# Down projection of a decoder step: twenty of its 43 row blocks by seven products, conv inputs loaded earlier

## The chip, the cores and the metric

The kernel runs on one core of one Trainium2 chip. The metric is the device time of one execution in microseconds (us), lower is better. TensorE (PE in the rows) does the matmuls, VectorE (DVE) and ScalarE (ACT) the elementwise work, GpSimd (POOL) some elementwise work and the DMAs that its software issues, and SyncE (SP) issues most of the other DMAs.

## The reference

One layer of a hybrid decoder for 544 tokens (512 of a prompt, 8 times 4 samples), width 2048, all in float32. A mixer (gated linear attention in 10 heads, dilated attention in 12) ends in an output projection and a residual `h`. Then comes the feed-forward part that the change is about, and a last RMSNorm:

```
up   = rmsnorm(h) @ w_up                    # 2048 -> 2 x 5504
conv = conv_b + sum(conv_w[j] * full[:, j:j+t] for j in 0..2)   # causal, width 3, history from state_ffn_conv
u, g = conv[..., :5504], conv[..., 5504:]
h    = h + (silu(g) * u) @ w_down           # 5504 -> 2048
y    = rmsnorm(h) * norm_final
```

The product with `w_down` has 43 blocks of 128 rows to sum over (k), 16 output tiles of 128 features (ot), and 544 tokens in two halves of 272.

## The kernel before

Every float32 operand is cut into a rounded high part (`hi`, by ACT) and a remainder (`lo`, by DVE: source minus `hi`); `split` does it (L190, L191). One product of a 128x128 weight block with 272 tokens is then three matmuls: hi*hi, hi*lo, lo*hi. Weights come as `raw` tiles of up to eight k blocks by DMA on SP and are split into `whi` and `wlo`, of which there are three buffers each; of `raw` there are three too.

The order of the stages is: input projection with the attention (to about 840 us of the span), output projection (`w_out`, to about 1061), up projection with conv and SiLU (to about 1985), down projection (the rest). A scheduler orders each engine's instructions by itself: blocks under `high_priority` (`ahead`, `evac`) are put forward by so many instructions, and a pool gives a buffer away only when its last reader is done. Each engine, and SP's and POOL's issuing of DMAs, runs its list strictly in order.

**Output projection.** The 16 normed head outputs `o[k]` are split into `ah`/`al` pairs (`act_pair`, one fixed buffer pair for each number); the pairs are those that held the input of the layer, which the last input tile still reads, k = 0 first. `order` sums o[10] to o[15] first. The residual rows `h` are loaded by POOL (L935) and added to the PSUM tile `g`, of which there are two.

**Up projection.** It already uses seven products instead of eight (Strassen's scheme in Winograd's form) for each pair of output tiles, pair of k blocks and the two token halves: `factors` makes seven right factors of the activations (B11, B21, B22, T1 to T4), `Pair` loads and adds the weight blocks. Sums of two weight blocks are made by a second DMA from POOL that adds into the tile (`accum_op`), others by DVE (L1013, L1034). `ra` and `rs` are the tiles of the first block and of the sum, with buffers of their own; the other three loads of a pair use `raw`. Before the first pair's conv, POOL loads `vcv` (conv weights, L1086) and `ci` (conv history, L1101) into the pool `FP`.

**Down projection.** The activations of each k block went to DRAM (`adr`), but for the three blocks of KEPT. The three KEPT blocks are multiplied first for all 16 tiles (L225, evacuated by ACT at L1156). The other 40 follow in groups of 16, 16 and 8: `fetch` loads a block into `ar` (L1141) and splits it into `dh`/`dl`, `gemm` (L225) runs over the group for each of the 16 tiles, DVE adds the PSUM tile to `h[ot]` (L1199) and, in the first group, the residual `hr` (L1203). Of the last group, the second eight tiles are done half by half so that the final norm of the first half runs beside the second.

Of the kernel before, what the change touches and what calls it, by code (L numbers as in the profile page):

```python
# [17 lines left out]
P = 128  # L18
# [27 lines left out]
NSLOT = 11  # L46
# [77 lines left out]
def _build(tc, nc, es, xT, st_gla, ck, cv, conv_in, vecs, w_in, w_gu, w_out, w_up, w_dn,  # L124
# [744 lines left out]
    for k in order:  # L869
        og[k] = act_pair(k)  # L870
        split(og[k][0], og[k][1], o[k])
# [23 lines left out]
    def factors(some, X, pool):  # L895
# [24 lines left out]
        for i in some:  # L920
            nc.vector.scalar_tensor_tensor(b[i][:, 2], b[i][:, 0], -1.0, b[i][:, 2], op0=OP.mult, op1=OP.subtract)
            if late:
                parts(i, T4, 1, b[i][:, 2:3])
            else:
                parts(i, T3, 2, b[i][:, 1:3])

# [158 lines left out]
    vcv = FP.tile([P, NVEC - V_CW], F32, name="vcv")  # L1085
    nc.gpsimd.dma_start(vcv, vecs[:, V_CW:])  # L1086

    ci_v = conv_in.rearrange("p (s f) r -> p s f r", s=2)
    co_v = conv_out.rearrange("p (s f) r -> p s f r", s=2)
# [5 lines left out]
    ci = co = None  # L1095
    for f, pr in enumerate(pairs):
        if f % 4 == 0:
            n = min(4, KF - f)
            ci = FP.tile([P, 2, 4, 2 * NB], F32, tag="ci", name="ci", bufs=2)
            co = FP.tile([P, 2, 4, 2 + 2 * NB], F32, tag="co", name="co", bufs=2)  # L1100
            nc.gpsimd.dma_start(ci[:, :, :n, :], ci_v[:, :, f:f + n, :])  # L1101
# [27 lines left out]
    ds_p, DS = opened(name="ds", bufs=NSLOT)  # L1129

    taken = [0]

    def slot(n=0):

        pool = DS2 if n else DS
        return pool.tile([P, NT], F32R, tag="dh", name="dh"), pool.tile([P, NT], F32R, tag="dl", name="dl")

    def fetch(k, n):
        hi, lo = slot(n)
        x = DS.tile([P, NT], F32, tag="ar", name="ar", bufs=2)  # L1140
        nc.sync.dma_start(x, adr[k])  # L1141
        split(hi, lo, x)
        return hi, lo

    h = [None] * KD
    A1 = {}
    rest = [k for k in range(KF) if k not in KEPT]
    groups = [rest[:16], rest[16:32], rest[32:]]
    with tc.high_priority(offset=min(1500, tc.cur_priority - P0)):
        for k in groups[0][:NSLOT]:  # L1150
            A1[k] = fetch(k, 0)
# [6 lines left out]
    ds2_p, DS2 = opened(name="ds2", bufs=24 - NSLOT, side="right")  # L1158
    w3_p, W3 = opened(name="w3", bufs=1, side="right")
    even = [0]  # L1160

    def wraw():
        even[0] ^= 1
        if even[0]:
            return wts.tile([P, 8, P], F32, tag="raw", name="raw", bufs=3)
        return W3.tile([P, 8, P], F32, tag="raw3", name="raw3", bufs=2)
# [4 lines left out]
    def wheld(w, ks, c0, n):  # L1171

        raw = wraw()
        wload(raw, w, ks, c0)
        out = []
# [146 lines left out]
```

## Time and profile before

| | |
|---|---|
| median of 3 runs | 2524.89 us (2522.66 to 2529.08) |
| the profiled execution, its own time | 2525.1 us |
| its span, first to last instruction | 2523.3 us |
| PE busy | 2462.7 us, 19479 matmuls |
| DVE, ACT, POOL busy | 1619.3, 1078.8, 435.3 us |
| mean granted TensorE clock | 0.991 of full |

The profiled execution lasted 1.8 us longer than its span and lies 0.2 us above the median. Busy time of PE is an upper bound of its useful time, since matmuls overlap in it; so the argument goes by how many matmuls pass in a stretch, and by the times at which PE waits.

### The profile page before, as it was taken

Reading aid. Unit: us, or ns where it says so; the run is one execution under the profiler, and the core shown is the slowest. Engines: PE = TensorE matmul, PEld = TensorE weight load, DVE = VectorE, ACT = ScalarE, POOL = GpSimd, SP = SyncE. Lnnn points to the kernel's source line nnn. Section 1 sums busy time; section 2 is a strip of 40 time slices with the busy share of each in tenths; the row PEclk is TensorE's granted clock in tenths of the full one; section 3 lists DMA queues with packets and bytes.
Section 4 is the critical chain, followed back from the end, with each engine's and each line's share of the span. In section 5 each row is a group of like instructions: output and inputs, shape, how many; then the busy total and the mean of one; then the engine's idle time right before and its main releaser. Section 6 shows DMA issues by size and latency. Waiting matters only on the chain.

```text
span 2523.3 us, 47163 instructions
## 1 busy us (share of the span) xinstructions
PE 2462.7 (98%) x19479; PEld 2385.2 (95%) x19479; DVE 1619.3 (64%) x2460; ACT 1078.8 (43%) x1870; POOL 435.3 (17%) x581
## 2 busy tenths in 40 slices
PE   8999999999999899989999999999999999999997
PEld 8988887899999899989999999999999999999997
DVE  7777764267777843478878888888888643342243
ACT  6344464133334433355555555555555531131142
POOL 1333434210002320112212221222121000000001
PEclk9999999999999999999999999999999999999999
DMA  7777744544555498668888888889888473443232
GB/s 220 197 202 197 193 114 138 161 131 141 166 177 177 159 305 256 169 146 192 192 188 192 191 191 189 191 191 192 189 191 178 124 219 107 115 151 92 85 100 72
DMA packets 581593, 427.73 MB, mean 170 GB/s; under 512 B 18976, under 2 KB 553728, under 8 KB 580608
## 3 DMA queue, kind: packets, MB, share of 16 engines
q1 hardware_dynamic: 462144, 248.31, 34.9%
q0 software_dynamic: 115200, 171.02, 30.1%
q10 hardware_dynamic: 4032, 5.38, 0.6%
q8 instruction: 153, 2.51, 0.4%
q14 instruction: 64, 0.52, 0.1%
HBM read 397.40 MB, written 77.37 MB: 188 GB/s over the span
## 4 chain that ended last, share of the span: by engine, by line
PE 82%; DMA 8%; DVE 6%; issue 2%; POOL 1%; ACT 1%; SPq 0%; DVEq 0%; POOLq 0%; ACTq 0%
PE g L225 40%; PE b L965 20%; PE g L965 15%; DMA q<-qscr 6%; DVE pr L411 1%; PE v L507 1%; PE s L673 1%; DMA ar<-adr 1%; DVE wlo L191 1%; DVE kv L412 1%; PE s L561 1%; DMA xr<-in_xT_dram 0%; PE s L548 0%; PE s L795 0%; POOL q L408 0%
## 5 line engine op out<-in xcount | busy, mean ns | idle before, releaser
L191 DVE TENSOR_TENSOR wlo<-raw,whi 128x1024 fp32r<-128x1024 f32 (+1 forms) x341 | 408.3, 1198 | 295.6 <-ACT whi L190 288.7
L190 ACT ACTIVATE whi<-raw 128x1024 fp32r<-128x1024 f32 (+1 forms) x345 | 355.0, 1030 | 555.1 <-PE g L225 454.0
L225 PE MATMUL g<-ah,whi 128*128 128x272 f32 x2048 | 442.9, 296 | 9.8 <-ACT ah L190 4.6
L225 PE MATMUL g<-al,whi 128*128 128x272 f32 x2048 | 447.2, 297 | 0.5 <-DVE al L191 0.5
L225 PE MATMUL g<-ah,wlo 128*128 128x272 f32 x2048 | 442.4, 295 | 0.3 <-DVE wlo L191 0.3
L965 PE MATMUL b<-vh,whi 128*128 128x272 f32 x1376 | 395.1, 288 | 6.2 <-ACT V L1038 4.8
L965 PE MATMUL b<-vl,whi 128*128 128x272 f32 x1376 | 395.9, 289 | 0.8 <-DVE vl L893 0.6
L965 PE MATMUL b<-vh,wlo 128*128 128x272 f32 x1376 | 389.9, 288 | 1.3 <-DVE wlo L191 1.3
L225 PEld LDWEIGHTS g<-ah,whi 128*128 128x128 f32 x2048 | 327.9, 191 | 19.7 <-issue 10.3
L225 PEld LDWEIGHTS g<-al,whi 128*128 128x128 f32 x2048 | 329.2, 191 | 11.6 <-issue 9.3
L225 PEld LDWEIGHTS g<-ah,wlo 128*128 128x128 f32 x2048 | 328.3, 190 | 10.2 <-issue 8.5
L965 PE MATMUL g<-vl,whi 128*128 128x272 f32 x1032 | 298.8, 290 | 2.0 <-DVE vl L893 1.9
L965 PE MATMUL g<-vh,whi 128*128 128x272 f32 x1032 | 297.8, 289 | 0.4 <-ACT vh L892 0.3
L965 PE MATMUL g<-vh,wlo 128*128 128x272 f32 x1032 | 296.8, 288 | 0.0
L965 PEld LDWEIGHTS b<-vh,whi 128*128 128x128 f32 x1376 | 260.0, 189 | 6.7 <-ACT V L1038 5.1
L225 PE MATMUL g<-dh,whi 128*128 128x272 f32 x1248 | 258.0, 288 | 4.1 <-ACT whi L190 2.7
L965 PEld LDWEIGHTS b<-vl,whi 128*128 128x128 f32 x1376 | 259.5, 189 | 1.5 <-DVE vl L893 1.5
L965 PEld LDWEIGHTS b<-vh,wlo 128*128 128x128 f32 x1376 | 257.4, 189 | 1.5 <-DVE wlo L191 1.5
L225 PE MATMUL g<-dh,wlo 128*128 128x272 f32 x1248 | 258.2, 288 | 0.0
L225 PE MATMUL g<-dl,whi 128*128 128x272 f32 x1248 | 258.1, 288 | 0.0
L190 ACT ACTIVATE whi<-rs 128x1024 fp32r<-128x1024 f32 x129 | 136.8, 1061 | 266.8 <-PE g L965 201.1
L225 PEld LDWEIGHTS g<-dh,whi 128*128 128x128 f32 x1248 | 195.7, 188 | 5.4 <-ACT whi L190 3.4
(341 smaller groups left out, 4101.5 us busy)
## 6 DMA issues: line engine op xcount, KB each, us to landing
raw<-in_w_up_dram SPq DMA_DIRECT2D x129, 512.0 KB, 4.1
raw<-in_w_in_dram SPq DMA_DIRECT2D x96, 512.0 KB, 4.8
raw<-in_w_dn_dram SPq DMA_DIRECT2D x64, 512.0 KB, 4.0
out_k_s_dram<-in_ck_dram POOLq DMA_DIRECT2D x8, 3060.0 KB, 12.7
out_v_s_dram<-in_cv_dram POOLq DMA_DIRECT2D x8, 3060.0 KB, 14.5
ra<-in_w_up_dram SPq DMA_DIRECT2D x43, 512.0 KB, 7.9
rs<-in_w_up_dram SPq DMA_DIRECT2D x43, 512.0 KB, 3.8
rs<-in_w_up_dram POOLq DMA_DIRECT2D x43, 512.0 KB, 9.8
```

The lines of the kernel that those rows point to most:

```text
L190: nc.scalar.activation(hi, src, AF.Copy)
L191: eng.tensor_sub(lo, src, hi.bitcast(F32))
L225: nc.tensor.matmul(ps[:, s, :HT], a, b[:, s * HT:(s + 1) * HT], start=(i == 0 and n == 0), stop=(i == len(todo) - 1 and n == 2))
L411: nc.vector.tensor_mul(pr, kt[:, 4:5, :].broadcast_to([P, TS, QC]), q5[:, 1:5, :])
L412: nc.vector.tensor_mul(kt[:, 0:4, :], kt[:, 0:4, :], q5[:, 0:1, :].broadcast_to([P, 4, QC]))
L507: nc.tensor.matmul(psv[32 * m:32 * m + 32, :QC], lhs, rhs, start=(kt == 0), stop=(kt == 5), tile_position=(0, 32 * m))
L561: nc.tensor.matmul(psc[r, :P], vt[:, j * P + 64 * e:j * P + 64 * e + 64], t[:, j * P:(j + 1) * P], start=(j == 0), stop=(j == qi))
L673: nc.tensor.matmul(ps[:, c * P:(c + 1) * P], KS[:, c * P:(c + 1) * P], Q[:, :, c * 64:(c + 1) * 64], start=True, stop=True)
L965: nc.tensor.matmul(b[:, :HT], a_[:, i, :], x_[i][:, v, :], start=(first and i == 0 and n == 0), stop=(i == 7 and n == 2), skip_group_check ...
```

## The change

1. The 40 other blocks of the down projection are now taken as 7 blocks as before, 10 blocks by seven products, 7 as before, 10 by seven products, and 6 as before at the end. In the ten-block stages each of eight pairs of output tiles (`Rows`) has seven products of 15 matmuls (five k pairs, three matmuls each). `right_factors` makes the factors of a k pair from two `ar` tiles into two `sv` tiles (10 of them); the weights come in tiles of five blocks (128x5x128), with `ra` and `rs` in two buffers each of their own and the other three loads of a pair from `raw`.
2. `og[k]` takes buffer pair n, its place in the order, instead of k.
3. `vcv`, `ci` and `co` move to the pool `wu`, and their first loads are written before the output projection.

```diff
-    for k in order:
-        og[k] = act_pair(k)
+    for n, k in enumerate(order):
+        og[k] = act_pair(n)
...
+    vcv = wu.tile([P, NVEC - V_CW], F32, name="vcv")
+    nc.gpsimd.dma_start(vcv, vecs[:, V_CW:])
...
+    def states(f):
+        n = min(4, KF - f)
+        ci = wu.tile([P, 2, 4, 2 * NB], F32, tag="ci", name="ci", bufs=2)
+        co = wu.tile([P, 2, 4, 2 + 2 * NB], F32, tag="co", name="co", bufs=2)
+        nc.gpsimd.dma_start(ci[:, :, :n, :], ci_v[:, :, f:f + n, :])
+        return ci, co
+    state = states(0)
...
-groups = [rest[:16], rest[16:32], rest[32:]]
+    NP2 = 5
+    plain = (others[:NSLOT], others[NSLOT + 2 * NP2:2 * NSLOT + 2 * NP2])
+    first_of = (NSLOT, 2 * NSLOT + 2 * NP2)
+    ks = others[2 * NSLOT + 4 * NP2:]
...
+    def right_factors(k):
+        x, y = astage(k), astage(k + 1)
+        H, L = stile(), stile()
+        b = [x[:, :HT], x[:, HT:], y[:, :HT], y[:, HT:]]
+        def two(v, src):
+            nc.scalar.activation(H[:, v], src, AF.Copy)
+            nc.vector.tensor_sub(L[:, v], src, H[:, v].bitcast(F32))
+        two(B11, b[0])
+        nc.vector.tensor_sub(b[0], b[0], b[1])
+        two(T1, b[0])
...
+    class Rows:
+        def load(self, *parts, x=None):
+            x = wraw()[:, :NP2] if x is None else x
+            for n, (side, t) in enumerate(parts):
+                c0 = (2 * self.o + side) * P
+                (nc.gpsimd if n else nc.sync).dma_start(x, self.w[t][:, :, c0:c0 + P], **({"accum_op": OP.add} if n else {}))
+        def p1(self):
+                self.a11 = self.load((0, 0), x=W3.tile([P, NP2, P], F32, tag="ra", name="ra", bufs=2))
...
+            self.product(self.b0, A_, B11)
+            nc.scalar.activation(self.V, self.b0[:, :HT], AF.Copy)
+        def others(self, then):
+                self.s = self.load((1, 0), (1, 1), x=W3.tile([P, NP2, P], F32, tag="rs", name="rs", bufs=2))
...
+            self.product(z, A_, T1)
...
+                nc.vector.tensor_add(self.s, self.s, self.a11)
+            self.product(self.b0, A_, T2, False)
...
+                a12 = self.load((0, 1))
+            self.product(y, A_, B21)
...
+                nc.vector.tensor_add(self.s, self.s, a12)
+                A_ = self.cut(self.load((0, 0), (1, 0)))
+            self.product(self.b0, A_, T3, False)
...
+            if then is not None:
+                then.p1()
...
+            self.product(z, A_, B22, False)
...
+                A_ = self.cut(self.load((1, 1)))
+            self.product(self.b0, A_, T4, False)
...
+    for gi in range(2):
+        for ot in range(KD):
+            gemm(ps, [wpart(w_dn, plain[gi], ot * P)], A)
...
+        rowpairs = [Rows(o_, first_of[gi], fac) for o_ in range(KD // 2)]
+        rowpairs[0].p1()
+        for i, rp in enumerate(rowpairs):
+            rp.others(rowpairs[i + 1] if i + 1 < len(rowpairs) else None)
```

Three places show how it moves instructions. The first is ACT at the first pair of the up projection; `F` is the tile whose history columns are filled from `ci`, `rstdF` the norm factors, `whi` the next weights, `V` an evacuation that PE waits for. Before:

```order
L190 ACTIVATE whi<-rs 128x1024
L1017 ACTIVATE U<-b_11320 128x272
L1082 ACTIVATE rstdF<-rstd 128x512
L1083 ACTIVATE rstdF<-rstd 128x8x4
L1028 ACTIVATE F<-ci 128x8x2 x2
L190 ACTIVATE whi<-raw 128x1024
L1038 ACTIVATE V<-b_11320 128x272
```

The same place now:

```order
L191 ACTIVATE whi<-rs 128x1024
L1033 ACTIVATE U<-b_11325 128x272
L1044 ACTIVATE F<-ci 128x8x2 x2
L1098 ACTIVATE rstdF<-rstd 128x512
L1099 ACTIVATE rstdF<-rstd 128x8x4
L191 ACTIVATE whi<-raw 128x1024
L1054 ACTIVATE V<-b_11325 128x272
```

The copies from `ci` stand two places earlier. Their load moved on POOL from behind the output projection to ahead of its first ten loads of `h`, which is where POOL now has:

```order
L773 DMA out_gla_s_dram<-S_8289 128x8x128
L635 DMA out_v_s_dram<-in_cv_dram 48x16320
L929 DMA vcv<-in_vecs_dram 128x344
L938 DMA ci<-in_conv_in_dram 128x2x64 x2
L951 DMA h<-in_xT_dram 128x544 x10
L1007 DMA rs<-in_w_up_dram 128x8x128
```

Three issues were put in between; nothing else moved on POOL there. The second place is PE at the start of the output projection, the last matmuls ahead of those that need the last two heads (`ah_9199`, `ah_9203`); `s<-sq,onesV` sums squares for the norm of these heads. Before:

```order
L781 MATMUL s<-sq,onesV 128x512
L225 MATMUL g<-ah_9187,wlo 128x272
L225 MATMUL g<-ah_9191,whi 128x272 x2
L225 MATMUL g<-al_9192,whi 128x272 x2
L225 MATMUL g<-ah_9191,wlo 128x272 x2
L225 MATMUL g<-ah_9195,whi 128x272 x2
L225 MATMUL g<-al_9196,whi 128x272 x2
L225 MATMUL g<-ah_9195,wlo 128x272 x2
L781 MATMUL s<-sq,onesV 128x64
L225 MATMUL g<-ah_9199,whi 128x272 x4
```

Now:

```order
L226 MATMUL g<-al_9196,whi 128x272 x2
L226 MATMUL g<-ah_9195,wlo 128x272 x2
L782 MATMUL s<-sq,onesV 128x512
L782 MATMUL s<-sq,onesV 128x64
L226 MATMUL g<-ah_9199,whi 128x272 x4
```

The 13 projection matmuls that stood between the two sums of squares now stand ahead of both. The third place is SP inside a ten-block stage, where one pair of output tiles is one round of five loads:

```order
L1211 DMA ra<-in_w_dn_dram 128x5x128
L1211 DMA raw<-in_w_dn_dram 128x5x128 x2
L1211 DMA rs<-in_w_dn_dram 128x5x128
L1211 DMA raw<-in_w_dn_dram 128x5x128
L1211 DMA ra<-in_w_dn_dram 128x5x128
```

Before, a pair of output tiles had four loads of 128x8x128 in these groups and no adding DMA; now, for ten blocks, it has five of 128x5x128 on SP and two adding ones on POOL.

## Rows read from the trace of the kernel before

**Rows 1.** The page: busy time of PE and POOL, and the chain that ended last.
```profile
PE 2462.7 (98%) x19479; PEld 2385.2 (95%) x19479; DVE 1619.3 (64%) x2460; ACT 1078.8 (43%) x1870; POOL 435.3 (17%) x581
PE 82%; DMA 8%; DVE 6%; issue 2%; POOL 1%; ACT 1%; SPq 0%; DVEq 0%; POOLq 0%; ACTq 0%
```
**Rows 2.** Windows: stretch, length, PE, PEld, DVE, ACT, POOL busy (instructions), clock, DMA share, GB/s.
```profile
1200.00:1900.00 700.00, 700.00 (x5598) 700.00 (x5598) 559.75 (x767) 360.31 (x633) 143.90 (x184) 1.00 0.89 191
2040.00:2400.00 360.00, 360.00 (x2880) 360.00 (x2879) 122.92 (x133) 81.61 (x88) 0.00 (x0) 1.00 0.41 119
```
**Rows 3.** Waits (us in total, times, longest) where the up projection starts; a window.
```profile
PE b L965 <- ACT V L1038: 4.8, 1, 4.8
ACT F L1028 <- DMA ci<-in_conv_in_dram: 4.8, 1, 4.8
1097.00:1102.00 5.00, 5.00 (x28) 5.00 (x28) 2.58 (x3) 0.71 (x3) 0.00 (x0) 0.63 1.22 237
```
**Rows 4.** Waits of PE and POOL around the start of the output projection; POOL's issues of `ci`.
```profile
PE g L225 <- ACT ah L190: 4.6, 1, 4.6
PE g L225 <- DVE h L936: 3.1, 1, 3.1
PE g L225 <- DVE al L191: 0.5, 1, 0.5
POOL h L935 <- issue: 17.3, 1, 17.3
L1101 POOL DMA_DIRECT2D ci<-in_conv_in_dram x2: 721/726/732, 1088.9 to 1089.7; - x2
```
**Rows 5.** Start of the down projection: the window, and what PE waited for in it.
```profile
1985.00:2040.00 55.00, 51.46 (x390) 50.39 (x389) 26.67 (x41) 29.86 (x53) 1.32 (x2) 0.97 0.75 215
PE g L225 <- ACT whi L190: 2.2, 2, 2.0
PE g L225 <- ACT h L1156: 1.4, 2, 1.1
```
**Rows 6.** Groups of instructions: busy us, mean ns of one, then idle before. Up projection, then down.
```profile
L1013 DVE TENSOR_TENSOR rs<-rs,ra 128x1024 f32<-128x1024 f32 x34 | 41.7, 1225 | 1.2
L1030 DVE TENSOR_TENSOR F<-g,V 128x272 f32<-128x272 f32 x33 | 14.3, 434 | 0.0
L1001 ACT ACTIVATE V<-b 128x272 f32<-128x272 f32 x34 | 12.9, 380 | 0.0
L191 DVE TENSOR_TENSOR wlo<-raw,whi 128x1024 fp32r<-128x1024 f32 x8 | 9.7, 1220 | 1.6 <-ACT whi L190 1.6
L191 DVE TENSOR_TENSOR wlo<-raw,whi 128x384 fp32r<-128x384 f32 x16 | 8.9, 555 | 5.0 <-ACT whi L190 4.9
L190 ACT ACTIVATE whi<-raw 128x384 fp32r<-128x384 f32 x16 | 8.3, 518 | 10.2 <-PE g L225 4.2 <-issue 2.8 <-PE g L965 2.4
L190 ACT ACTIVATE whi<-raw 128x1024 fp32r<-128x1024 f32 x8 | 8.2, 1046 | 1.1 <-DMA raw<-in_w_dn_dram 1.1
```
**Rows 7.** Timeline of SP and POOL over one pair of the up projection.
```profile
1501.25 0.37 SPq L989 DMA_DIRECT2D ra<-in_w_up_dram  x1
1522.26 0.37 SPq L989 DMA_DIRECT2D ra<-in_w_up_dram  x1
1508.33 2.88 SPq L989 DMA_DIRECT2D raw<-in_w_up_dram  x2
1515.36 1.60 POOL L991 DMA_DIRECT2D raw<-in_w_up_dram  x1 [2.89 <-DMA raw<-in_w_up_dram]
```
**Rows 8.** DMA issues, KB each, median us to landing: up projection (1200 to 1900), then down.
```profile
raw<-in_w_up_dram SPq DMA_DIRECT2D x100, 512.0 KB, 4.1
raw<-in_w_up_dram POOLq DMA_DIRECT2D x34, 512.0 KB, 7.0
rs<-in_w_up_dram POOLq DMA_DIRECT2D x34, 512.0 KB, 9.9
raw<-in_w_dn_dram SPq DMA_DIRECT2D x55, 512.0 KB, 4.0
```

More of the change, by code (lines that the diff above doesn't have):

```diff
@@ L45 @@
 NKEPT = 3
-NSLOT = 11
+NSLOT = 7
+NAR = 2
 FW = 2 + TP + NB * (2 + TS)
@@ L1094, in _build @@
     kept = {}
-    ci = co = None
     for f, pr in enumerate(pairs):
         if f % 4 == 0:
[L1098 to L1101, printed above, removed]
+            ci, co = states(f) if f else state
         pr.ci, pr.co = ci[:, :, f % 4, :], co[:, :, f % 4, :]
@@ L1129, in _build, with late, astage, fetch @@
     ds_p, DS = opened(name="ds", bufs=NSLOT)
[L1131 to L1140, printed above, removed]
-        nc.sync.dma_start(x, adr[k])
-        split(hi, lo, x)
-        return hi, lo
-    h = [None] * KD
-    A1 = {}
-    rest = [k for k in range(KF) if k not in KEPT]
-    groups = [rest[:16], rest[16:32], rest[32:]]
-    with tc.high_priority(offset=min(1500, tc.cur_priority - P0)):
-        for k in groups[0][:NSLOT]:
-            A1[k] = fetch(k, 0)
+    h = [None] * KD
+    others = [k for k in range(KF) if k not in KEPT]
+    NP2 = 5
+    plain = (others[:NSLOT], others[NSLOT + 2 * NP2:2 * NSLOT + 2 * NP2])
+    first_of = (NSLOT, 2 * NSLOT + 2 * NP2)
+    ks = others[2 * NSLOT + 4 * NP2:]
+    assert len(ks) <= NSLOT
+    def late(n=2000):
+        return tc.high_priority(offset=min(n, tc.cur_priority - P0))
+    def astage(k):
+        x = DS.tile([P, NT], F32, tag="ar", name="ar", bufs=NAR)
+        nc.sync.dma_start(x, adr[k])
+        return x
+    def fetch(k):
+        hi = DS.tile([P, NT], F32R, tag="dh", name="dh")
+        lo = DS.tile([P, NT], F32R, tag="dl", name="dl")
+        split(hi, lo, astage(k))
+        return hi, lo
+    with late():
+        A = {k: fetch(k) for k in plain[0]}
     for ot in range(KD):
@@ L1173, in wheld, with wsplit2 @@
+    def wsplit2(raw):
+        hi = wts.tile([P, 8, P], F32R, tag="whi", name="whi")
+        lo = wts.tile([P, 8, P], F32R, tag="wlo", name="wlo")
+        split(hi[:, :NP2], lo[:, :NP2], raw)
+        return hi, lo
+    def wheld(w, ks, c0):
+        m = len(ks)
         raw = wraw()
         wload(raw, w, ks, c0)
-        out = []
-        for j in range(2):
-            hi, lo = [t[:, :4 * P].rearrange("p (k c) -> p k c", k=4) for t in slot(n[j])]
-            r = raw[:, 4 * j:min(4 * j + 4, len(ks)), :]
-            m = r.shape[1]
-            split(hi[:, :m], lo[:, :m], r)
-            out.append([(ks[4 * j + x], hi[:, x, :], lo[:, x, :]) for x in range(m)])
@@ L1182, in wheld @@
[L1182 to L1203 removed]
+        t = stile().rearrange("p a b -> p (a b)")
@@ L1241, in _build @@
     for i in range(HK):
-        held.append(wheld(w_dn, ks, (HK + i) * P, [pool_of[(used + 2 * i + j) % 24] for j in range(2)]))
+        held.append(wheld(w_dn, ks, (HK + i) * P))
     for s in range(2):
```

108 lines of the change are left out of this document (75 added, 33 removed).

## The prediction

> **What bounds the kernel now.** I read the page first: TensorE is busy for 98% of the span and holds 82% of the chain that ended last [rows 1]. Busy time is no peak, so I then took the windows. In the middle of the up projection and of the down projection PE has no idle time at all, and the number of matmuls per us is the same: 5598 in 700 us and 2880 in 360 us, that is 125.0 ns for each matmul with its own weight load [rows 2]. So in these stretches the time is the count of matmuls times 125 ns, unless another engine or a load falls behind. What the reader should see beside it: VectorE is busy for 560 of the 700 us and the DMA engines for a share of 0.89 in the up projection, and that does not hold PE up; in the down projection both are far lower (123 of 360 us, 0.41). That room is what the change spends. PE idles only at the joints of the stages, and there I read the waits: the start of the up projection, of the output projection, and of the down projection [rows 3 to 5].
>
> **The matmuls.** Before, the down projection has 43 blocks x 16 tiles x 6 matmuls = 4128. Now: 3 kept blocks 3 x 16 x 6 = 288; twice seven plain blocks 2 x 7 x 16 x 6 = 1344; twice ten blocks by seven products 2 x 8 pairs x 7 x 15 = 1680; six last blocks 576; together 3888. That is 240 fewer, all in stretches where nothing but PE ended the time: 240 x 125.0 ns = **-30.0 us** [rows 2]. The Trainium skill (TensorE: Matmul & The Clock Gate, Back-to-back issue gap) gives columns/2.4 + 2.5 ns for a warm matmul, 115.8 ns at 272 columns; by that the saving would be an estimated 27.8 us. The trace does not agree by 9 ns each, and the row decides.
>
> **The conv inputs.** At the first pair ACT waited 4.8 us for the load of `ci` with the next weights and the evacuation `V` queued behind it, and PE waited 4.8 us for that `V` [rows 3]. PE had been running until then and came back at a granted clock of 0.63 over the next 5 us, partly at the lower of its two levels (1.2 and 2.4 GHz): 28 matmuls where 125 ns each would give 40, 1.5 us lost [rows 3]. With `ci` there long before, the copies into `F` stand ahead of `rstdF` and wait only for `F`'s own memory, which comes free when the factors are done. I take **-6.3 us**; the bounds are 0 (if that memory frees as late as the load landed) and -6.3. Next in line are `rstdF` and the weight split, which ACT reached before the wait anyway.
>
> **The output projection's start.** PE waits 4.6 us for the splits of the last two heads and 3.1 us for DVE's add, behind which a load of `h` is late [rows 4]. The order shows the same 168 projection matmuls (two tiles, 14 of 16 blocks, six each) ahead of the last heads as before, so the first wait is not removed by the buffers: what it waits for is the chain of these heads. What can go are small waits on splits, 0.5 us the largest [rows 4]. On the other side the second sum of squares now stands behind 13 more matmuls, up to 13 x 0.125 = 1.6 us later for the chain. POOL issues three more DMAs ahead of `h`, at 0.73 us each 2.2 us [rows 4]; it had sat idle for 17.3 us before them, so they are covered unless their memory frees as late as `h`'s. Bounds -4.6 and +3.8; I take **0**, since gain and loss are of one size and the chain itself is unchanged.
>
> **The start of the down projection.** Over 55 us 390 matmuls pass where 440 would: 6.2 us lost, of which 3.6 us are waits, 2.2 for weight splits by ACT [rows 5]. Sixteen blocks were fetched there through two `ar` buffers, and a split that waits for such a load holds the weight splits behind it. Now seven are fetched there: I take half of the loss away, -3. But seven are fetched at the head of the first ten-block stage and six at the second, again on ACT between weight splits; I charge the longest such wait seen, 2.0 us, at each, +4. Together **+1 us**, bounds -6 and +12 (6.2 at both heads).
>
> **Inside the ten-block stages.** One pair of output tiles is 105 matmuls, 13.1 us of PE. DVE has seven splits of 640 elements (between the 555 ns of 384 and the 1220 of 1024, 0.82 us), two adds of the same size (1225 at 1024, so 0.82) and seven adds from PSUM at 434 ns: 10.4 us. ACT has seven splits (between 518 and 1046, 0.73) and three evacuations at 380 ns: 6.3 us [rows 6]. Both fit, in about the proportion of the up projection. The loads are five on SP and two adding ones on POOL of 320 KB in 13.1 us, where the up projection has the same seven of 512 KB in 21.0 us [rows 7]: the same bytes per us, without its writes of activations, so a share at or below 0.89 [rows 2], which PE there did not feel. What is new is the latency: the buffer that takes a load and an added load must go round in 13.1 us instead of 21.0. In the trace the second `raw` load is issued by 1511.2, POOL adds to it from 1515.4 [rows 7], the added part lands 7.0 us later [rows 8], and ACT and DVE split it in 1.05 and 1.22 us [rows 6]: 13.4 us at 512 KB. With 5/8 of the bytes it is somewhere between 5/8 of each step, 8.4 us, and the whole 13.4. I take the middle, under 13.1, and **0 us**; the upper bound is 16 pairs x 0.3 = +5.
>
> **Covered elsewhere.** A seven-block tile is 5.25 us of PE against one split of 896 elements (under 1.22 us) and two adds; the factors of five k pairs are 55 DVE instructions of 434 ns, 24 us within 84 us of PE. If DVE fell behind there, the first product would wait; I see no reason. The tail behind the last matmul is not touched.
>
> **Sum.** 2525.1 (the profiled execution, 0.2 above the median) - 30.0 - 6.3 + 0 + 1 + 0 = **2490 us**.
>
> **The rivals.** *A: the feed binds a little.* The round trip of the added block is 13.1 to 15.3 us; at 14, 16 x 0.9 = 14 us are given back: 2504. For it: 13.4 at full size, and that lists on SP and POOL are strict, so one late load delays the next. Against: PE's idle time of zero in 700 us at the same byte rate. Chance 0.18. *B: the feed binds hard, and the change is slower.* Place: the same buffer. If the added part takes the 9.9 us that the up projection's `rs` adds took [rows 8], the round trip is 16.3 us, 3.2 us over, 16 times: 51 us, 2541. It decides against the change from 35 / 16 = 2.2 us over, a round trip of 15.3. Against: smaller transfers, and the `raw` adds took 7.0. The Trainium skill (DMA: Bandwidth & Descriptors, Latency and other measured facts) reports that copies from HBM slow down at large powers of two between rows, 207 GB/s at 512 KiB and 164 at 2 MiB; taking every second block puts the five blocks 2 MiB apart, where they stood 1 MiB apart. By that rule the load and add would take 1.26 times as long, an estimate. Nothing in the trace bears it out: at 1 MiB a `w_dn` load lands in 4.0 us, a `w_up` load, without such a distance, in 4.1 [rows 8]. As a mechanism of this kernel, 1.26 times the 11.2 us of the full-size round trip gives 16.4 us, and again some 2541; of 5/8 it gives 10.3 and changes nothing. Chance of B, by either way, 0.06. *C: the joints cost more.* ACT's splits of fetched blocks hold up weights at both heads and at both ends of the ten-block stages, 3 us more at each: +12, 2502. Chance 0.10. *D: the early loads do not do what they say.* `F` frees no earlier and the output projection loses its 3.8 us: +10, 2500. Chance 0.08. My forecast has the rest, 0.58, between 2482 and 2498.
>
> **The numbers.** What a measurement of this kernel tells from no change is about 0.3%, 7.6 us, so faster is below 2517. Forecast, C and D are faster (0.76), and of A's 0.18 0.14 are; same is A's remaining 0.04; slower is B's 0.06. The range runs from 2482 (no cost at the heads, and the 4.6 us gone) to 2512: it leaves out B, the upper third of A, and some 0.04 below.
>
> **What would show it.** Right: 3888 matmuls in the down projection; a window inside a ten-block stage with PE without idle time at 125 ns each, DVE near 10 of every 13 us, DMA share 0.8 to 0.9; no wait for `V` behind `ci`; waits for `ah` and `h` still there. A and B would show as PE waiting, once in every 13 us, for a split of `raw`, with ACT idle until the added DMA lands. C would show as waits in the first 20 us of each ten-block stage. The forecast is wrong if the ten-block stages run at more than 13.5 us a pair.

## The result and the profile after

| | before | after |
|---|---|---|
| median of 4 runs each, us | 2525.6 (2522.7 to 2529.1) | 2500.9 (2498.8 to 2503.3) |
| the profiled execution, span | 2523.3 | 2498.6 |

The ratio is 0.990 with a 95% interval of 0.9888 to 0.9911. The change is faster by 24.7 us where 35 were forecast. It lies in the range, 11 us above the forecast value and 2.9 us above the 2482 to 2498 that the prediction kept for its forecast. The direction and the largest term were right; about a third of the gain went somewhere else, and the rest of this text looks for it.

The page after, busy time and the chain that ended last. It answers to [rows 1]: 240 matmuls fewer, as counted, and DVE's share up from 64 to 70%.

```profile
PE 2436.3 (98%) x19239; PEld 2359.9 (94%) x19239; DVE 1754.3 (70%) x2766; ACT 1146.8 (46%) x2040; POOL 484.3 (19%) x613
PE 79%; DMA 10%; DVE 4%; issue 4%; POOL 2%; ACT 1%; SPq 0%; DVEq 0%; ACTq 0%; POOLq 0%
```

Windows of the changed kernel (columns as in [rows 2]): the first 50 us of the up projection; its middle; 55 us from the start of the down projection; the first ten-block stage; the second seven-block stage; the second ten-block stage.

```profile
1063.70:1113.70 50.00, 43.24 (x302) 40.88 (x301) 43.14 (x82) 32.15 (x66) 6.59 (x9) 0.93 0.61 137
1200.00:1900.00 700.00, 700.00 (x5568) 700.00 (x5568) 558.67 (x765) 358.98 (x631) 141.58 (x182) 1.00 0.88 190
1986.30:2041.30 55.00, 52.63 (x406) 52.19 (x406) 31.05 (x55) 30.54 (x58) 4.45 (x4) 0.97 0.79 218
2110.40:2218.20 107.80, 106.62 (x846) 106.18 (x845) 81.61 (x132) 52.01 (x88) 21.63 (x15) 1.00 0.86 186
2218.30:2301.80 83.50, 83.50 (x670) 83.50 (x669) 50.84 (x92) 28.45 (x51) 2.45 (x2) 1.00 0.47 128
2301.80:2409.80 108.00, 106.97 (x847) 106.32 (x846) 80.48 (x131) 51.25 (x85) 19.60 (x13) 1.00 0.76 161
```

The first 50 us of the up projection in the kernel before, for the same comparison:

```profile
1061.40:1111.40 50.00, 38.69 (x256) 35.59 (x255) 37.96 (x76) 27.74 (x59) 7.40 (x9) 0.90 0.57 124
```

Three things stand here. The joint at the first pair is better: 302 matmuls pass instead of 256, 46 x 0.125 = 5.8 us. The middle of the up projection, which no edit touched, is **slower**: 5568 matmuls in 700 us where [rows 2] had 5598, with PE busy all the time, the clock at full and the DMA share no higher. That is 125.7 ns a matmul instead of 125.0, and over the 7224 matmuls of the stage 4.8 us. And in the ten-block stages 846 and 847 matmuls (four of the next stage among them, and a few that only overlap an edge of the window) take 107.8 and 108.0 us, where 844 of 125 ns make 105.5; PE idles for 1.2 and 1.0 us in them. Without the four that is 13.4 us a pair of tiles, just below the 13.5 that I had named as the limit.

PE's waits in the changed kernel, from the output projection through the start of the up projection, then in the down projection (us in total, times, longest). They answer to [rows 3 to 5].

```profile
PE g L226 <- ACT ah L191: 4.8, 1, 4.8
PE g L226 <- DVE h L952: 4.0, 1, 4.0
PE b L981 <- ACT V L1054: 0.8, 1, 0.8
...
PE g L226 <- ACT h L1166: 2.4, 2, 2.0
PE g L226 <- DVE h L1333: 1.7, 2, 1.1
PE b L1221 <- ACT whi L191: 1.1, 1, 1.1
PE g L1221 <- ACT whi L191: 0.9, 1, 0.9
```

The wait for `V` behind `ci` fell from 4.8 to 0.8 us [rows 3]. The wait for `ah` is where it was, and the one for `h` rose from 3.1 to 4.0 [rows 4]. In the down projection there are waits for `h`, evacuated by ACT at the start and added by DVE at the end, and one wait in each ten-block stage.

Stage by stage, from the start of a stage's first matmul to that of the next stage's, in us. The first column is when the output projection reaches its 169th matmul; the last is the time from there to the end of the span. The first column scatters by up to 9 us between executions of kernels that do not differ there (878.0 in best2, 887.4 in after_again; 882.7 and 887.4 in two profiles of the changed kernel), so small differences are read from the stages and not from the medians. Four matmuls of the next stage fall into a ten-block stage.

| kernel | reaches | output | up | to 1st ten | ten | seven | ten | six and tail | from there |
|---|---|---|---|---|---|---|---|---|---|
| before | 881.6 | 179.8 | 923.7 | | | | | 538.2 in all | 1641.8 |
| early_only | 881.9 | 179.7 | 922.6 | | | | | 538.1 in all | 1640.5 |
| after | 882.7 | 181.0 | 922.6 | 124.0 | 107.9 | 83.6 | 107.9 | 88.9 | 1615.9 |
| after_again | 887.4 | 180.5 | 922.7 | 125.9 | 107.6 | 83.6 | 108.0 | 88.9 | 1617.1 |
| after_oldpair | 880.9 | 180.5 | 922.6 | 123.7 | 106.7 | 83.5 | 109.5 | 88.9 | 1615.5 |
| after_pad32 | 882.8 | 180.9 | 917.8 | 124.0 | 106.5 | 83.6 | 106.4 | 88.9 | 1608.1 |
| after_pad_both | 878.9 | 180.9 | 916.5 | 126.0 | 107.7 | 83.6 | 107.1 | 88.9 | 1610.6 |
| after_w0 | 883.2 | 180.7 | 918.0 | 123.2 | 108.1 | 83.7 | 106.8 | 88.9 | 1609.5 |
| best1 | 884.1 | 178.8 | 918.0 | 126.2 | 106.6 | 83.6 | 107.9 | 89.3 | 1610.2 |
| pad_both_own | 883.8 | 181.0 | 916.5 | 126.6 | 108.4 | 83.6 | 107.1 | 88.8 | 1611.9 |
| swap | 881.4 | 180.3 | 916.5 | 122.5 | 106.8 | 83.6 | 106.6 | 88.7 | 1604.9 |
| best2 | 878.0 | 179.2 | 916.5 | 121.8 | 106.9 | 83.6 | 108.0 | 89.0 | 1604.8 |
| feed2 | 884.8 | 180.1 | 916.5 | 125.8 | 106.1 | 83.6 | 106.9 | 92.2 | 1611.1 |

### The profile page after: what moved, and what is told of

It is laid out like the page before. It is cut to its first block, busy times and chain, and to the rows that moved or that the text cites. A ratio compares the mean times of both kernels' runs of the same rounds, so it can differ in the third digit from the quotient of the medians.

```text
span 2498.6 us, 47520 instructions
## 1 busy us (share of the span) xinstructions
PE 2436.3 (98%) x19239; PEld 2359.9 (94%) x19239; DVE 1754.3 (70%) x2766; ACT 1146.8 (46%) x2040; POOL 484.3 (19%) x613
## 4 chain that ended last, share of the span: by engine, by line
PE 79%; DMA 10%; DVE 4%; issue 4%; POOL 2%; ACT 1%; SPq 0%; DVEq 0%; ACTq 0%; POOLq 0%
PE g L226 30%; PE b L981 20%; PE g L981 16%; DMA q<-qscr 6%; PE b L1221 3%; DMA raw<-in_w_dn_dram 3%; PE g L1221 2%; PE v L508 1%; PE s L674 1%; DVE pr L412 1%; PE s L562 1%; DVE wlo L192 1%; PE s L549 1%; DVE kv L413 0%; ACT whi L191 0%
## 5 line engine op out<-in xcount | busy, mean ns | idle before, releaser
L192 DVE TENSOR_TENSOR wlo<-raw,whi 128x1024 fp32r<-128x1024 f32 (+4 forms) x357 | 403.5, 1131 | 219.4 <-ACT whi L191 207.9
L191 ACT ACTIVATE whi<-raw 128x1024 fp32r<-128x1024 f32 (+4 forms) x361 | 351.7, 975 | 435.0 <-PE g L226 260.8
L191 ACT ACTIVATE whi<-rs 128x1024 fp32r<-128x1024 f32 (+1 forms) x177 | 172.3, 974 | 318.2 <-PE g L981 203.4
L192 DVE TENSOR_TENSOR wlo<-rs,whi 128x1024 fp32r<-128x1024 f32 (+1 forms) x177 | 197.3, 1114 | 37.1 <-ACT whi L191 35.3
L981 PEld LDWEIGHTS g<-vl,whi 128*128 128x128 f32 x1032 | 195.7, 190 | 2.9 <-DVE vl L894 2.9
L981 PEld LDWEIGHTS g<-vh,whi 128*128 128x128 f32 x1032 | 195.2, 189 | 0.7 <-ACT whi L191 0.6
L981 PEld LDWEIGHTS g<-vh,wlo 128*128 128x128 f32 x1032 | 195.8, 190 | 0.0
```

What stands on the lines that cost most here:

```text
L191: nc.scalar.activation(hi, src, AF.Copy)
L192: eng.tensor_sub(lo, src, hi.bitcast(F32))
L981: nc.tensor.matmul(b[:, :HT], a_[:, i, :], x_[i][:, v, :], start=(first and i == 0 and n == 0), stop=(i == 7 and n == 2), skip_group_check ...
```

## The experiments

### Where the up projection lost its pace

The theory came from the built program: the early table adds 3552 bytes to the pool `wu`, and the right factors of the first four pairs of k blocks lie behind it. `vh0` starts at byte 129376 before, 32 past a multiple of 64, and at 125824 after, a multiple of 64. Right factors `vh4` to `vl7` are at multiples of 64 in both, the weights `whi` and `wlo` 32 past one in both.

**early_only** is the kernel before with the early table and nothing else (and `NSLOT` 10, for the space):

```diff
-NSLOT = 11
+NSLOT = 10
...
+    vcv = wu.tile([P, NVEC - V_CW], F32, name="vcv")
+    nc.gpsimd.dma_start(vcv, vecs[:, V_CW:])
...
+    state = states(0)
```

> The kernel before with the early table alone (vcv, ci and co in wu; NSLOT 10 instead of 11 in the down projection, since the space is gone; the same 4128 matmuls). Theory: the table has two effects of opposite sign. It takes away the wait for V behind ci (4.8 us, about 6 us with the slow matmuls behind it), and its 3552 bytes in wu move the first four pairs of right factors (vh, vl) to other start addresses, at which a matmul of the up projection takes 125.75 ns instead of 125.1: four pairs (168 matmuls each) every 84.5 us instead of 84.05, +4.8 us over the stage. Together about -1 us: 2522 to 2527, with 5565 to 5570 matmuls in 700 us of the up projection. Rival 1: the slower matmuls belong to the other parts of the change (or to that execution) and the table is worth its 6 us: 2517 to 2521, 5595 to 5600 matmuls in 700 us. Rival 2: the table gains nothing even at the joint.

Measured: 2524.4 us, ratio 1.0005 (0.9996 to 1.0014). Two windows of it, the first 50 us and the middle of the up projection:

```profile
1061.60:1111.60 50.00, 43.30 (x302) 40.79 (x301) 43.15 (x82) 32.17 (x66) 6.66 (x9) 0.93 0.61 136
1200.00:1900.00 700.00, 700.00 (x5569) 700.00 (x5568) 558.40 (x761) 357.38 (x627) 140.51 (x182) 1.00 0.88 190
```

Both effects are there without any of the new down projection: 302 matmuls in the first 50 us, and 5569 in 700. The table won 5.8 us at the joint and lost nearly all of it along the stage, so the stage as a whole gained 1.1 (923.7 to 922.6), and nothing of it can be measured in the end.

**after_pad32** puts the factors back 32 bytes, **after_pad_both** moves the other four pairs as well:

```diff
-    vcv = wu.tile([P, NVEC - V_CW], F32, name="vcv")
+    vcv = wu.tile([P, NVEC - V_CW + 8], F32, name="vcv")
...
     ra_p, RA = opened(name="ra", bufs=1)
+    RA.tile([P, 8], F32, name="pad")
```

The first hunk is after_pad32 (with the load into `vcv[:, :NVEC - V_CW]`), both together are after_pad_both.

> The changed kernel with the tile vcv 32 bytes longer, nothing else: the right factors vh0 to vl3 (and sv and most ra, rs) start 32 bytes past a multiple of 64 again, as in the kernel before, vh4 to vl7 stay at a multiple of 64. Theory (start addresses set the pace): matmuls of the up projection fall back to 125.1 ns, about 5597 in 700 us, four pairs every 84.05 us; -4.5 to -5.5 us, 2495 to 2497 beside a 2501 of the changed kernel. Rival (the pace belongs to the order or to the traffic of the new kernel): no difference within 1 us, 2500 to 2502, 5566 in 700 us.

> As the one before, and a tile of 32 bytes at the head of the pool RA, so that vh4 to vl7 too start 32 bytes past a multiple of 64. Theory: in the kernel before, matmuls whose right factor started at such an address took 124.7 ns against 125.4 for the others; so all would take 124.7: 20.95 us a pair against 21.13, about 5610 in 700 us, -7.5 us against the changed kernel, 2492 to 2495. Rival 1 (what counts is that the two halves lie differently, as in the kernel before): as the run with one pad, 2495 to 2497, or back at 2501. Rival 2 (no matter of addresses): 2500 to 2502.

Measured: 2493.4 us (0.9878; 0.9865 to 0.9892) and 2491.4 us (0.9870; 0.9857 to 0.9884). The middle of the up projection with one pad and with both:

```profile
1200.00:1900.00 700.00, 700.00 (x5599) 700.00 (x5598) 558.91 (x766) 359.93 (x633) 141.79 (x182) 1.00 0.89 191
```

```profile
1200.00:1900.00 700.00, 700.00 (x5607) 700.00 (x5606) 560.93 (x768) 362.18 (x634) 140.20 (x181) 1.00 0.89 191
```

With one pad the pace of the kernel before is back, and the stage is 4.8 us shorter, as expected. With both it is faster than it ever was, 6.2 us shorter than in the changed kernel (7.5 expected). Both medians lie below what was expected (2495 to 2497, and 2492 to 2495). The rest of the gain with one pad is in the ten-block stages, 2.9 us for both: the pad also moves `sv` off the multiples of 64, and their matmuls, leaving out gaps, went from 125.7 and 125.6 to 125.1 and 125.0 ns from start to start, some 0.5 us a stage; the rest is that no wait fell into the middle of a stage in that execution. I had not counted either.

**after_w0** asks whether it is the place of the moving data alone, or against the weights:

```diff
+    pad_p, PAD = opened(name="pad", bufs=1, side="right")
+    PAD.tile([P, 8], F32, name="pad")
     wts_p, wts = opened(name="wts", bufs=3, side="right")
```

(with the longer `vcv` as well, so that of the matmuls' operands in the up projection only the weights change their place modulo 64).

> The changed kernel with 32 bytes put ahead of the pool of the weights and 32 more in vcv: raw, whi and wlo, which started 32 bytes past a multiple of 64 in every kernel so far, now start at a multiple of 64, and all right factors stay at a multiple of 64 as in the changed kernel. Theory 1 (what counts is how the weights lie against the moving data; different is slow): all matmuls of 272 columns get the pace of the padded version, 124.9 ns: the up projection -6 us, the ten-block stages -1 us, and the input and output projections, whose moving data lie at a multiple of 64 in every kernel, gain up to 0.6 ns a matmul too, -2 to -4 us: 2488 to 2493. Theory 2 (what counts is where the moving data lie by themselves): 2499 to 2502, 5566 in 700 us. Theory 3 (weights at a multiple of 64 are worse still): slower than 2502.

Measured: 2493.8 us (0.9876; 0.9861 to 0.9891). Two windows, the output projection and the up projection, and the first of them in the changed kernel:

```profile
900.00:1050.00 150.00, 150.00 (x1189) 150.00 (x1189) 62.79 (x85) 52.86 (x71) 14.18 (x24) 1.00 0.82 254
1200.00:1900.00 700.00, 700.00 (x5607) 700.00 (x5607) 559.57 (x768) 359.75 (x633) 142.40 (x184) 1.00 0.89 192
```

```profile
900.00:1050.00 150.00, 150.00 (x1197) 150.00 (x1196) 62.81 (x85) 52.99 (x71) 14.15 (x24) 1.00 0.82 252
```

The up projection got the full pace, 5607, with all factors at the place modulo 64 that they have in the changed kernel: so it is how weights and moving data lie against each other. But theory 1 went too far, and its 2488 to 2493 was missed. The output projection, in the changed kernel 1197 matmuls in these 150 us, is slower with 1189. There each weight block is used for two matmuls in turn, one for each token half, where the up projection changes weights at every matmul. The loss is small: in the second seven-block stage, where weights serve two matmuls as well, it is 601 instead of 602 in 75 us, and the output projection as a whole took 180.7 us, no longer than the 181.0 of the changed kernel: its start went better (393 matmuls instead of 389 from 895 to 945 us). For the up projection it holds that start addresses modulo 64, of which 0 and 32 were tried, set some 0.9 ns of a matmul, and that the better choice there was not the better one in the output projection. What the memory does there is not shown by these runs.

The addresses modulo 64 are not all of it. In the run swap, below, factors and weights lie 32 past a multiple of 64 in both ten-block stages, and PE is never idle in these windows, one in the first stage and one in the second:

```profile
2115.00:2190.00 75.00, 75.00 (x600) 75.00 (x599) 57.00 (x94) 33.90 (x56) 16.45 (x11) 1.00 0.89 183
2305.00:2380.00 75.00, 75.00 (x602) 75.00 (x602) 56.64 (x94) 34.10 (x56) 16.45 (x11) 1.00 0.87 174
```

From start to start that is 125.5 and 125.0 ns. What makes the difference stays open.

### The freed buffers and the output projection

**after_again** is the changed kernel itself, **after_oldpair** has `act_pair(k)` again:

```diff
-    for n, k in enumerate(order):
-        og[k] = act_pair(n)
+    for k in order:
+        og[k] = act_pair(k)
```

> The changed kernel with act_pair(k) as before instead of act_pair(n). Theory: the freed buffers neither gain nor lose, since the output projection's first wait is for the chain of the last heads; 2499.5 to 2502, and the waits of PE for ah (4.6 to 4.8 us) and for h (3 to 4 us) stay. Rival 1: the 1.2 us that the output projection became longer by come from act_pair(n), whose second sum of squares stands behind 13 more matmuls: this version is 1 to 1.5 us faster. Rival 2: the freed buffers did gain, and this version loses 1 to 4 us.

> The changed kernel itself, beside the others of this call on one chip. 2498 to 2502, and 5565 to 5570 matmuls in 700 us of the up projection. If it comes out near 2497, the 3.5 us between it and the version with act_pair(k) were those of the chip and not of the buffers.

Measured: 2497.4 us (0.9891; 0.9876 to 0.9906) for after_oldpair, 2502.4 us (0.9909; 0.9894 to 0.9924) for after_again. Whether the chip explains the gap between the medians is not settled: the two ran on different chips, and after_oldpair's did not run the changed kernel; the kernel before took 2524.1 us on after_oldpair's and 2524.9 on after_again's. The intervals overlap, and from the output projection on the profiles take 1615.5 us with the old pairs and 1615.9 and 1617.1 with the new: two profiles of one kernel differ by more than the versions. In the profiles the rest lies ahead of that point, in the part that scatters. PE's waits in after_oldpair:

```profile
PE g L226 <- ACT ah L191: 4.5, 1, 4.5
PE g L226 <- DVE h L952: 3.9, 1, 3.9
```

Both waits stay with either order of buffers. One wait goes with the new pairs: in the changed kernel PE waits 0.9 us for the second sum of squares, just ahead of the point where the table's count begins, and in after_oldpair it does not:

```profile
PE s L782 <- ACT sq L780: 0.9, 1, 0.9
```

It does not show in the time. From a run of 56 matmuls of the input projection (at 829.4 us in the changed kernel) to that point it is 53.3 us in after, 52.6 in after_again and 53.2 in after_oldpair. So the buffers neither gain nor lose anything that can be seen; and the higher wait for `h` is not theirs.

It is the table's. POOL in the changed kernel, where [rows 4] had it idle until it issued `h`:

```profile
882.90 0.59 POOL L929 DMA_DIRECT2D vcv<-in_vecs_dram  x1 [13.56 <-DVE oa L823]
883.49 1.45 POOL L938 DMA_DIRECT2D ci<-in_conv_in_dram  x2
884.93 3.73 POOL L951 DMA_DIRECT2D h<-in_xT_dram  x7
```

The 17.3 us of POOL's idle time did not cover the three loads, because their memory, too, came free only at 882.9. **best1** has both pads, the old pairs, and SP as the issuer of `vcv` and the first `ci` (the second `ci` stays on POOL):

```diff
-    nc.gpsimd.dma_start(vcv, vecs[:, V_CW:])
+    nc.sync.dma_start(vcv[:, :NVEC - V_CW], vecs[:, V_CW:])
...
-        nc.gpsimd.dma_start(ci[:, :, :n, :], ci_v[:, :, f:f + n, :])
+        (nc.gpsimd if f else nc.sync).dma_start(ci[:, :, :n, :], ci_v[:, :, f:f + n, :])
```

> The changed kernel with both pads, act_pair(k) as before, and the first loads of vcv and ci issued by SP instead of POOL. Theory: POOL's three loads ahead of the residual rows h made these 1.45 us later, and PE's wait for DVE's h rose from 3.1 us to 3.7 to 4.8; without them it is back at 3.1, and the output projection at 179.7 us instead of 180.8. With the pads' 8 to 9 us: 2489 to 2491, where the version with both pads alone took 2491.4. Rival: SP's loads delay the weights of the up projection behind them instead, and the wait at the first pair's V comes back: 2491 to 2496.

Measured: 2493.9 us (0.9870; 0.9854 to 0.9887). PE's wait for `h` is 3.3 us, and the output projection takes 178.8 us, the shortest of all. POOL's issue of `h` there shows when the memory of `h` itself comes free:

```profile
885.98 4.27 POOL L951 DMA_DIRECT2D h<-in_xT_dram  x8 [0.98 <-DVE al L192]
```

PE reached the last heads at 884.05 us in best1 and at 882.71 in the changed kernel. So `h` can be issued 1.9 us behind that point (as in the kernel before), and the three loads made it 2.2: only 0.3 us are POOL's list. DVE's add of the first `h` came 8.7 us behind the point instead of 7.4, since the loads landed later too (medians of 7.0 us instead of 6.7); the rest of this delay is not taken apart.

As a whole the version does not beat after_pad_both: the up projection is 1.5 us longer, with slightly longer waits for `vl` (2.2 us against 1.9) and `wlo` (1.3 against 1.0) at its start. That is the rival's size, but not its mechanism, since the wait for `V` did not come back (0.8 us). best2, below, has the same loads without that loss, so the loss goes with the old pairs or with the execution; which one was not tried.

### The ten-block stages and their start

**pad_both_own** gives the block to which POOL adds one buffer of its own:

```diff
-                A_ = self.cut(self.load((0, 0), (1, 0)))
+                A_ = self.cut(self.load((0, 0), (1, 0), x=W3.tile([P, NP2, P], F32, tag="rx", name="rx", bufs=1)))
```

> The version with both pads, with one buffer of its own for the block to which POOL adds (name rx; the other two loads of a pair of output tiles keep the three raw buffers). It asks for the cost of the feed in the ten-block stages, where PE waited 0 to 2 times in a stage, 1.1 to 1.4 us each, for the split of a raw tile whose added part came late. Theory: the added load no longer waits for the buffer of an ordinary one, the waits in the middle of the stages go, 106.0 to 106.6 us a stage instead of 106.4 to 109.5; -1 to -3 us, 2488 to 2491. Rival: with one buffer the round trip is longer than 13.1 us (load 4, add 7.3, split 1.6, and POOL's 1.5 of issue make 14.4), PE waits in every pair: +1 us a pair, 2500 to 2515.

Measured: 2498.2 us (0.9888; 0.9873 to 0.9902). Neither came: the stages took 108.4 and 107.1 us, with two waits of together 1.2 us in the middle of the first. The round trip of this block in the changed kernel shows why (SP's issue, POOL's adding issue, ACT's split, SP's next issue, and the split two pairs on):

```profile
2143.20 0.37 SPq L1211 DMA_DIRECT2D raw<-in_w_dn_dram  x1
...
2147.99 1.51 POOL L1211 DMA_DIRECT2D raw<-in_w_dn_dram  x1 [9.08 <-DMA raw<-in_w_dn_dram]
...
2155.32 0.74 ACT L191 ACTIVATE whi<-raw 128x640 fp32r<-128x640 f32 x1 [2.19 <-DMA raw<-in_w_dn_dram]
...
2156.95 0.37 SPq L1211 DMA_DIRECT2D raw<-in_w_dn_dram  x1
...
2184.18 0.74 ACT L191 ACTIVATE whi<-raw 128x640 fp32r<-128x640 f32 x1 [4.63 <-DMA raw<-in_w_dn_dram]
```

From 2143.20 to 2156.95 it is 13.75 us. That exceeds PE's 13.1 to 13.2 us for a pair by half a us, ACT's slack shrinks, its wait grows to 4.63 us, and then PE waits once (the 1.1 us above). One private buffer has about the same round trip: in pad_both_own it is loaded anew every 11.8 to 15.2 us in the first stage, 13.5 on average, and every 13.2 on average in the second. **swap** and **best2** turn to the start of the down projection first, **feed2** comes back to this.

**swap** has both pads and opens two pools in the other order, which lays `ra`, `rs` and `hr` on memory that comes free later, in part that of the KEPT blocks; **best2** is swap with SP as the issuer of the table, as in best1:

```diff
-    w3_p, W3 = opened(name="w3", bufs=1, side="right")
     sv_p, SV = opened(name="sv", bufs=2 * NP2, side="right")
+    w3_p, W3 = opened(name="w3", bufs=1, side="right")
```

> The version with both pads, with the pools W3 (ra, rs and hr of the down projection) and SV opened in the other order, so that W3 lies on the memory of the KEPT blocks and its loads can't start before these are multiplied. Theory: at the start of the down projection four loads and two added loads of 320 KB for the first ten-block stage, wanted 125 us later, and two of hr stand ahead of the first ar loads; these landed after 6 to 7 us instead of 3, ACT waited for them 2.8 us with the evacuation h behind, and PE for h once or twice, 2.1 us each, at half clock afterwards. With the early loads held back the first ar loads land in 3 to 4 us, no wait for h over 1 us is left, and the part from the KEPT blocks to the first ten-block stage takes 121 to 123 us instead of 124 to 126: 2488 to 2490 where the version with both pads alone took 2491.4. Rival: ACT waits for ar anyway, since there are two ar buffers and the split must have one back; 123.5 to 126 us as before.

> As swap, with the first loads of vcv and ci issued by SP instead of POOL; act_pair(n) as in the changed kernel. Theory: both joints gain, the output projection 1 to 2 us (178.8 to 179.8 us instead of 180.9), the start of the down projection 2 to 3: 2486 to 2489. Rival: as in the run with act_pair(k) and SP, 1.5 us of it come back as waits for vl and wlo at the first pair of the up projection: as swap, 2488 to 2490.

Measured: 2488.3 us (0.9861; 0.9846 to 0.9875) and 2486.9 us (0.9858; 0.9841 to 0.9874). SP in the changed kernel at the start of the down projection:

```profile
1985.05 0.47 SPq L1211 DMA_DIRECT2D ra<-in_w_dn_dram  x1
1985.60 0.48 SPq L1211 DMA_DIRECT2D rs<-in_w_dn_dram  x1
1986.13 0.52 SPq L1211 DMA_DIRECT2D ra<-in_w_dn_dram  x1
1986.70 0.52 SPq L1211 DMA_DIRECT2D rs<-in_w_dn_dram  x1
1987.26 1.47 SPq L1151 DMA_DIRECT2D ar<-adr  x1
```

and in swap:

```profile
1978.31 0.82 SPq L1152 DMA_DIRECT2D ar<-adr  x2
1979.34 2.05 SPq L847 DMA_DIRECT2D raw<-in_w_dn_dram  x2
...
2014.49 0.43 SPq L1212 DMA_DIRECT2D ra<-in_w_dn_dram  x1
```

How the `ar` loads landed that were issued up to 2000 us of the span, changed kernel and swap (KB each, median us to landing):

```profile
ar<-adr SPq DMA_DIRECT2D x4, 272.0 KB, 6.9
```

```profile
ar<-adr SPq DMA_DIRECT2D x9, 272.0 KB, 2.8
```

The loads that were wanted 125 us later went first because their memory was free first. Held back, `ar` lands in 2.8 us, PE's waits of 2.0 us for ACT's `h` are gone (what is left in swap are waits for DVE's `h`, 1.1 us at the longest), and the part up to the first ten-block stage takes 122.5 and 121.8 us instead of 123.2 to 126.6. feed2, with the same order of the pools, took 125.8, with a wait that is told there. best2's output projection takes 179.2 us, and its wait for `h` is 3.1 us, the value of the kernel before. best2 is the fastest version of all; against swap it is not told apart by the medians.

**feed2** is best2 with two `rx` buffers and, for the space, one buffer `c` instead of two:

```diff
-                A_ = self.cut(self.load((0, 0), (1, 0)))
+                A_ = self.cut(self.load((0, 0), (1, 0), x=W3.tile([P, NP2, P], F32, tag="rx", name="rx", bufs=2)))
...
-        return W3.tile([P, NT], F32, tag="c", name=name, bufs=2)
+        return W3.tile([P, NT], F32, tag="c", name=name, bufs=1)
```

> The version best2 with two buffers of their own (rx) for the block to which POOL adds, and for the space one buffer instead of two for hr and the squares of the last norm (tag c). It asks again for the cost of the feed in the ten-block stages. In the trace of the changed kernel this block's round trip is 13.2 to 13.8 us (issued by SP at 2143.20, landed at 2147.3, added from POOL at 2147.99, landed at 2155.2, split until 2156.9, issued again at 2156.95), some tenths of a us longer than the 13.1 us that PE takes for a pair; ACT's wait for it grows from 1.6 to 4.6 us over five pairs, and then PE waits once, 1.1 us. With one buffer of its own the round trip is the same, and so were the waits. Theory: with two buffers the round trip may take 26 us, and no wait of over 0.3 us is left in the middle of the ten-block stages: 105.9 to 106.7 us each with the waits at head and end; 2484 to 2487.5 where best2 took 2486.9, if the single buffer c costs under 1 us. Rival 1: the waits in the middle come from the DMA engines' load, not from the buffer, and stay (0 to 2 a stage, 1 us each). Rival 2: the single hr buffer holds DVE up in the first seven-block stage, 16 times up to 0.5 us: 2488 to 2495, visible as PE's waits for h there.

Measured: 2493.6 us (0.9875; 0.9859 to 0.9892), slower than best2. The stages took 106.1 and 106.9 us, with no wait over 0.3 us in the middle of either; what is left is at their heads and ends. That alone would prove little, since swap (106.8 and 106.6 us) and after_pad32 had no wait in the middle either, without such buffers. What shows the theory at work is ACT: its waits for tiles of `raw`, the added block among them, in the first ten-block stage of the changed kernel are the row below (swap has 14.1 us there); in feed2 there is no such row for any weight block.

```profile
ACT whi L191 <- DMA raw<-in_w_dn_dram: 18.6, 9, 4.6
```

The price was elsewhere, as rival 2 said in kind but not in place. PE's waits in feed2 from 1900 us to the end:

```profile
PE g L226 <- ACT sv L1185: 3.4, 1, 3.4
PE g L226 <- DVE h L1334: 3.2, 2, 2.0
```

The single `c` holds the last norm's squares up (six and tail: 92.2 us instead of 89.0), and in the first seven-block stage PE waited once, 3.4 us, behind a factor split of ACT; whether that is the single buffer's doing, too, was not tried. A feed worth 2 us at most (213.0 us for both stages against 214.9 in best2 and 213.4 in swap) was bought with a buffer worth at least 3.

## Why the prediction was right, and where it was off

**The range held, in part by luck.** 2500.9 lies above the 2482 to 2498 of the forecast, where rivals C and D had put 2502 and 2500. Neither is what happened: against D the wait for `V` went, and against C the heads cost 0.3 and 1.1 us and the ends nothing that shows, not 3 at each of four places. The largest part of the difference, 4.8 us of pace, stood in no rival and in no term; the range covered it because it was wide enough for A.

**Right: the matmuls, -30.0 us.** 240 fewer, in stretches at 125 ns: the window of the second seven-block stage has 670 in 83.5 us with PE never idle. The prices of DVE and ACT in a pair of tiles were right as well: splits and adds of 640 elements took 0.82 us on DVE and 0.74 on ACT.

**Half right: the conv inputs, -6.3 us.** The wait went and the joint gained 5.8 us. The step that failed is the unspoken one under it, in the first paragraph: that a stretch with PE always busy costs "the count of matmuls times 125 ns". That 125 was a property of where the tiles lay, and the moved table moved them. +4.8 us, which two runs undo (after_pad32, after_w0) and one makes by itself (early_only). This is the largest part of the missing 11. The Trainium skill (SBUF — State Buffer, Operand start alignment) asks for a start at a multiple of the element size and says of it "This is about legality, not speed", with runs that "timed nothing"; here 32 bytes were worth 4.8 us of 922.6.

**Off by 1.2: the output projection, 0 us.** The bounds held it. The condition that I had named (covered unless the table's memory frees as late as `h`'s) came near: it freed 1.7 us before that of `h`, the three loads took 2.0, and `h` was issued 0.3 us later. DVE's add came 1.3 us later, and PE waited 0.9 us more. Most of that is the later landing of `h`, which I had not priced; I had priced POOL's issue alone. That the freed buffers change nothing was right; the 13 more matmuls before the second sum of squares show as a wait of 0.9 us ahead of it, but not in the time.

**Off by about 1: the down projection's start and the heads, +1 us.** Over 55 us 406 matmuls pass instead of 390 [rows 5], 2.0 us won where I took 3. At the heads of the ten-block stages one matmul came 0.3 us late in the first and 1.1 in the second, rather than 2.0 each. What held the start up was not fetched blocks alone, as in rival C, but early loads ahead of them on SP and POOL, which I had not looked for.

**Off by 1.5: inside the ten-block stages, 0 us.** The round trip was to lie in the middle between 8.4 and 13.4 us; in the rows shown it was 13.75, beyond the upper end. The added load landed after 7.2 us at 320 KB where 512 KB took 7.0 [rows 8]: I had let latency shrink with the bytes. (For the adds into `rs` it did shrink, from 9.9 to 7.4 us.) So rival A was the truth in kind, at a tenth of its price, since the excess is half a us and slack takes it up for some pairs: one wait of 1.1 us in the first stage, one of 0.3 in the second. Rival B's 16.4 us did not come. Whether the wider distance between blocks has a part in these 7.2 us no run separates. The rule that the prediction drew on (the Trainium skill, DMA: Bandwidth & Descriptors, Latency and other measured facts) is on the pitch between the rows of neighbouring partitions in copies between HBM tensors, 207 GB/s at 512 KiB and 164 at 2 MiB; here 2 MiB lie between blocks of one partition, so it is not the same case. The two stages took 4.8 us more than their matmuls at 125 ns in all: 3.5 are these waits and the heads, with the slower matmul behind each, and the rest is the pace of `sv` at multiples of 64, some 0.6 us each.

**Not in the sum: the last stage.** With six blocks instead of eight a tile gives PE less time, and the splits of held weights and the last additions by DVE cost 1.7 us of waits; the last 288 matmuls took 39.1 us instead of 36.9.

**The account.** The sum was -35.3 us, the two profiles differ by -24.7. Of the 10.6 us between them 5.2 are the up projection's (4.8 of pace, the rest at the joint), 1.2 the output projection's, 3.5 the down projection's (-25.5 where -29 was the sum), and 1.1 lie ahead of the output projection, within the scatter of that part; the tail behind the last matmul gave 0.4 back.

## What to carry to other kernels

A tile that is added or moved shifts every tile behind it in its pool's stack: after any such change, count matmuls in a window of a stage that was not touched, and if the pace moved, try 32 bytes of padding before looking for anything else. A load that waits for nothing but memory is issued as soon as the memory is free, however late it is wanted; lay it on memory that comes free when it should start. For a feed with an adding DMA, do not count on a shorter latency for a smaller block: take that of the trace at full size as the estimate, and compare the round trip of one buffer with the time in which it must come back.

## What was unexpected of the hardware

The pace of a matmul of 272 columns with its own weights was 125.7, 125.0 or 124.8 ns in the up projection (5568, 5598 and 5607 in 700 us), when nothing but the start addresses of right factors and weights was moved, by 32 bytes. With both operands at the same place modulo 64 (0 or 32) the up projection was fastest, whichever place that is; for the output projection, which uses weights twice, the same step cost 8 matmuls in 1197. In swap the ten-block stages differ (125.5 and 125.0 ns) with the same places modulo 64, so this is not the whole rule. An adding DMA of 320 KB from POOL into `raw` landed no sooner than one of 512 KB (7.2 and 7.0 us); into `rs` it did (7.4 and 9.9).
